# The second feed-forward layer's input half as seven products of quarters

## The chip, the cores and the metric

The kernel runs on one core of one Trainium2 chip. The metric is the device time of one execution in microseconds (us). The core has a matrix engine (TensorE, PE in the profile; PEld is its loading of stationary operands), a vector engine (VectorE, DVE), an activation engine (ScalarE, ACT), GpSimd (POOL) and a queue that starts transfers (SyncE, SP). SBUF is the working memory of 128 partitions; PSUM, eight banks of 128 x 512 float32, takes what TensorE accumulates.

## The reference, cut to what matters

Two layers run over 512 latent tokens of width 1024. Each has a token mixer (layer 0 attention, layer 1 a chunked gMLP), then a gated feed-forward layer. The change touches the last of these, in layer 1:

```
FFN_HIDDEN = 2816
def swiglu(h, w_in, w_out):
    gate, up = jnp.split(h @ w_in, 2, axis=-1)
    return (jax.nn.silu(gate) * up) @ w_out
...
f_l = swiglu(modulate(rmsnorm(x, norm_g[i, 2]), sh_fl, sc_fl), ffn_w_in[i], ffn_w_out[i])
x = x + g_fl * rmsnorm(f_l, norm_g[i, 3])
```

## The kernel before

**Numbers.** Every large product keeps float32 accuracy by three fp32r matmuls. An operand is split into a high part, `high`, a cast on ACT (L195), and a low part, `low`, the difference on DVE (L198). The three products are hi·hi, hi·lo and lo·hi.

**The feed-forward layer's input half** (class `FFN`). The hidden width 2816 is 22 units of 128 columns. A unit's weights are 128 gate and 128 up columns for all 1024 inputs: one raw tile of 1 MB (`w_raw`, two buffers), fetched by SP, and split in two halves into `w_hi` and `w_lo` (four buffers each). `H` holds the layer's input turned to features x tokens, high parts in its first eight blocks and low parts in its last eight. Units 0 and 1 (weight units 55 and 56) are done token by token in `head`, while the mixer's output product still runs. Units 2 to 21 (weight units 57 to 76) are done in `rest`: for gate and for up, eight blocks of 128 inputs, three matmuls of 512 tokens each (L1302, L1303, L1304), so 48 matmuls a unit. `gated` takes the silu on ACT (L1282) and multiplies on DVE (L1283). A background generator `ada` builds one modulation vector during the first of these units: eight multiply-adds on DVE (L335), two broadcast sums on PE.

**What comes before and after.** `down` is an output product with its norm and residual chain: for each of the four token tiles it ends with `work` for the last weight units, then the `Chain` steps: square on ACT, gain (L1096), add to x (L1100), the gain for the next layer on POOL (L1112), shift on DVE (L1116), `turn` on PE (L1123), and the turned tile split into `H` on ACT and DVE. `head` (L239 to L241, `fa`) and `head_turn` (L1276, L1277) are laid among these steps. Two calls matter: the mixer's `down(GO, ...)`, which leads into the feed-forward layer, and the last `down`, the output half, which follows it and ends the program.

**What sets the order.** Inside `down` the steps are registered with `at(time, step)`, and `run_plan` issues them in the order of a hand-kept list of names, `ORDER`, or, for steps it does not name, by that time. The times are places in an order only. Each engine then works its own queue in that order, and semaphores between the engines hold the dependences. In `rest` the order is that of the code.

Of the kernel before, what the change touches and what calls it, by code (L numbers as in the profile page):

```python
# [181 lines left out]
def backbone_kernel(ctx: ExitStack, tc: tile.TileContext, a, out):  # L182
# [46 lines left out]
    def big(name):  # L229
        return base.tile([P, 2 * D], F32, name=name, tag="big", bufs=2)  # L230

# [86 lines left out]
    class Ada:  # L318
# [14 lines left out]
        def add(self, k, c0=0, c1=D):  # L333
            w, ac = self.raws[k // 2][:, (k % 2) * D + c0:(k % 2) * D + c1], self.acc[:, c0:c1]
            nc.vector.scalar_tensor_tensor(out=ac, in0=w, scalar=sc[:, k:k + 1], in1=ac, op0=ALU.mult, op1=ALU.add)  # L335

# [723 lines left out]
    def slot(name):  # L1060
        return psM_p.tile([P, D], F32, name=name, tag="b2", bufs=4)
# [76 lines left out]
    def down(u0, nu, lhs, G_of, nxt_of, head, bg=None, lend=None, part={}, yslot=lambda t: slot(f"y{t}")):  # L1138


        ps, sts = {}, {}
# [9 lines left out]
        def work(v, t, ns=(0, 1)):  # L1151
            v0 = 2 if t in part else 0
            if v < v0:
                return
            if v == v0:
                ps[t] = yslot(t)
            parts = ws.unit(u0 + v)
            for h in range(2):
                k = 2 * v + h
                st = sts[k]  # L1160
                mm_a(ps[t], st[:, t * P:(t + 1) * P], st[:, 512 + t * P:512 + (t + 1) * P], *parts[h],
                     k == 2 * v0, k == nk - 1, ns)

        ws.unit(u0)
# [16 lines left out]
        for t, c in enumerate(ch):  # L1181
            b = W * (t + 1)
            if nxt is None and t == NT - 1:
# [19 lines left out]
            if nxt is None:  # L1203
                at(b + 3.7, c.store)
                continue
# [5 lines left out]
        if nxt is not None:  # L1211
# [10 lines left out]
            for i in range(6):  # L1222
# [3 lines left out]
                at(b + 1, ws.low, u, h, nc.vector)  # L1226
        with tc.manual_schedule():
            run_plan()
    class FFN:
# [55 lines left out]
        def rest(self, nxt_of, head, bg=None):  # L1285
            H, prev = self.H, None
            if head is None:
                psM.__exit__(None, None, None)
                psE = pool("psE", space=PSUM)
                pe = psE.__enter__()  # L1290
                self.slot = lambda name: pe.tile([P, D], F32, name=name, tag="b2", bufs=3)
                self.bank = lambda name: pe.tile([P, 512], F32, name=name, tag="b1", bufs=2)
# [30 lines left out]
            if head is None:  # L1323
                down(F2[self.layer], NFF // 2, lhs, lambda: V[self.layer, 5], nxt_of, head, yslot=lambda t: (
                    self.slot(f"y{t}") if t < NT - 1 else tuple(self.bank(f"y{t}{n}") for n in range(2))))
                psE.__exit__(None, None, None)
            else:
                down(F2[self.layer], NFF // 2, lhs, lambda: V[self.layer, 5], nxt_of, head, bg, self.lend)
# [144 lines left out]
    f1 = FFN(1, ada(1, (5,), lambda name: f1.bank(name)))  # L1473
# [7 lines left out]
    down(GO, 4, lambda k: staged(uTs[k]), lambda: V[1, 2], lambda: (V[1, 4], V[1, 3], H2), f1.head, lend=open_f1)  # L1481
    f1.rest(lambda: None, None)
# [80 lines left out]
```

## Time and profile before

| | us |
|---|---|
| median of 3 runs (1169.78 to 1170.39) | 1169.95 |
| the profiled execution, its own time | 1170.17 |
| its span in the profile | 1168.4 |
| PE busy in the span | 1152.3 |
| DVE, ACT, POOL busy | 647.5, 450.4, 192.0 |
| the mixer's `down` with `head`, about | 785 to 823 |
| input half of the last feed-forward layer, units 2 to 21 | 823.04 to 1042.08 |
| its output half | 1042.08 to 1162 |
| end of the last chain and stores | 1162 to 1168.4 |

A row of a timeline gives a start, a duration, the engine, the line and the operation with its tile names; a square bracket gives the idle time before it and what ended it. Matmuls are pipelined: their own durations overlap, so the time one costs is read from start to start.

### The profile page before, as it was taken

The numbers are of one execution on the slowest core, as the hardware profiler recorded it, in microseconds if no ns is written. First come the engines' busy times: TensorE is split into PE (matmuls) and PEld (weight loads), VectorE is DVE, ScalarE is ACT, GpSimd is POOL, SyncE is SP. The second block draws the span as 40 slices with busy tenths as digits, with TensorE's granted clock in tenths as the row PEclk, the third lists the DMA queues.
The fourth block names the chain that finished last, engine by engine and source line by source line (L and its number), as shares of the span: only waits on it lengthen the run. The fifth ranks groups of instructions, "written<-read, shape, count | busy, mean of one in ns | idle before, by whom it ended". The sixth has DMA issues, their size and how long they took to land.

```text
span 1168.4 us, 14727 instructions
## 1 busy us (share of the span) xinstructions
PE 1152.3 (99%) x5918; PEld 954.8 (82%) x5918; DVE 647.5 (55%) x915; ACT 450.4 (39%) x723; POOL 192.0 (16%) x181
## 2 busy tenths in 40 slices
PE   8999999999999999999999999999999999999997
PEld 5789887778988888888888788889788888888886
DVE  6778989857454657634445755547453223223324
ACT  6357778655222222332324454245122222222322
POOL 2347576515000000000001322013000000000000
PEclk9999999999999999999999999999999999999999
DMA  9633222341254575633344243221352232232221
GB/s 370 264 134 124 85 97 73 109 172 63 99 195 175 185 284 216 250 111 127 125 144 144 95 159 126 73 72 73 134 218 95 95 108 94 87 108 94 87 72 72
DMA packets 24711, 157.97 MB, mean 135 GB/s; under 512 B 3258, under 2 KB 3514, under 8 KB 7364
## 3 DMA queue, kind: packets, MB, share of 16 engines
q1 hardware_dynamic: 24644, 157.04, 37.3%
q8 instruction: 46, 0.75, 0.3%
q14 instruction: 21, 0.17, 0.0%
HBM read 154.94 MB, written 2.10 MB: 134 GB/s over the span
## 4 chain that ended last, share of the span: by engine, by line
PE 91%; DVE 3%; DMA 2%; POOL 1%; ACT 1%; issue 1%; DVEq 0%; POOLq 0%; SPq 0%; ACTq 0%
PE y L247 25%; PE f L1302 12%; PE f L1304 12%; PE f L1303 12%; PE v L247 3%; PE o_ps L915 2%; PE pT_ps L895 2%; DMA ada<-in_ada 2%; PE s_ps L861 2%; PE s_ps L862 1%; PE q_ps L239 1%; PE u L1454 1%; PE u L1456 1%; PE u L1455 1%; PE q_ps L241 1%; PE q_ps L240 1%
## 5 line engine op out<-in xcount | busy, mean ns | idle before, releaser
L198 DVE TENSOR_TENSOR w_lo<-w_raw,w_hi 128x1024 fp32r<-128x1024 f32 x149 | 182.2, 1230 | 319.0 <-ACT w_hi L195 317.4
L195 ACT CAST w_hi<-w_raw 128x1024 fp32r<-128x1024 f32 x162 | 168.6, 1052 | 469.8 <-PE f L1303 247.1
L1302 PE MATMUL f<-H,w_hi 128*128 128x512 f32 x640 | 249.5, 390 | 1.5 <-DVE act L1277 1.5
L247 PE MATMUL y<-w_hi,st 128*128 128x512 f32 x928 | 250.9, 390 | 0.0
L1304 PE MATMUL f<-H,w_lo 128*128 128x512 f32 x640 | 249.1, 389 | 0.0
L1303 PE MATMUL f<-H,w_hi 128*128 128x512 f32 x640 | 249.0, 389 | 0.0
L247 PEld LDWEIGHTS y<-w_hi,st 128*128 128x128 f32 x928 | 173.7, 188 | 35.9
L247 PE MATMUL y<-w_lo,st 128*128 128x512 f32 x464 | 143.5, 389 | 0.0
L335 DVE SCALAR_TENSOR_TENSOR acc<-ada_raw,sc,acc 128x1024 f32<-128x1024 f32 x80 | 104.5, 1306 | 69.9 <-DMA ada_raw<-in_ada 68.8
L1302 PEld LDWEIGHTS f<-H,w_hi 128*128 128x128 f32 x640 | 120.1, 188 | 26.5 <-DVE act L1277 1.7
L1304 PEld LDWEIGHTS f<-H,w_lo 128*128 128x128 f32 x640 | 120.1, 188 | 25.1
L1303 PEld LDWEIGHTS f<-H,w_hi 128*128 128x128 f32 x640 | 120.2, 188 | 25.0
L223 POOL TENSOR_TENSOR ry<-ry,mhalf 128x1 f32<-128x1 f32 x16 | 10.1, 633 | 584.3 <-DVE ry L220 580.9
L247 PEld LDWEIGHTS y<-w_lo,st 128*128 128x128 f32 x464 | 87.1, 188 | 18.1
L889 POOL TENSOR_SCALAR p<-p,st 128x512 f32<-128x512 f32 (+1 forms) x64 | 55.8, 888 | 43.9 <-DVE st L885 26.6
L868 DVE CUSTOM_DVE_ANT_0 s_ps<-s_ps,mask,nsink 128x512 f32<-128x512 f32 (+1 forms) x64 | 51.8, 816 | 11.5 <-PE s_ps L862 9.2
L873 ACT ACTIVATE p<-s_ps,st 128x512 f32<-128x512 f32 (+1 forms) x64 | 47.6, 744 | 20.6 <-DVE st L868 16.9
L198 POOL TENSOR_TENSOR w_lo<-w_raw,w_hi 128x512 fp32r<-128x512 f32 (+1 forms) x23 | 37.8, 1653 | 29.5 <-ACT w_hi L195 29.5
L326 POOL MEMSET acc<- 128x1024 f32 x10 | 9.5, 955 | 201.8 <-DVE acc_st L198 200.3
L895 PE MATMUL pT_ps<-ident,p 128*128 128x128 f32 x288 | 42.3, 274 | 0.0
L861 PE MATMUL s_ps<-khi,qT 128*128 128x256 f32 (+1 forms) x128 | 40.8, 330 | 1.5 <-ACT p L873 0.8
L1112 POOL TENSOR_TENSOR tmp<-x,row 128x1024 f32<-128x1024 f32 x12 | 31.8, 2650 | 32.7 <-DVE x L1100 24.9
(208 smaller groups left out, 1679.5 us busy)
## 6 DMA issues: line engine op xcount, KB each, us to landing
w_raw<-in_w SPq DMA_DIRECT2D x87, 1024.0 KB, 4.8
ada_raw<-in_ada SPq DMA_DIRECT2D x40, 1024.0 KB, 4.8
ada<-in_ada SPq DMA_DIRECT2D x8, 1024.0 KB
row<-in_norm_g SPq DMA_DIRECT2D x7, 512.0 KB, 5.6
xin<-in_x SPq DMA_DIRECT2D x4, 512.0 KB, 5.7
x<-in_x SPq DMA_DIRECT2D x4, 512.0 KB, 3.9
out<-x SPq DMA_DIRECT2D x3, 512.0 KB, 2.6
xin<-in_ctx SPq DMA_DIRECT2D x2, 512.0 KB
```

What stands on the lines that cost most here:

```text
L195: nc.scalar.copy(out=hi, in_=src)
L198: (eng or nc.vector).tensor_tensor(out=lo, in0=src, in1=hi.bitcast(F32), op=ALU.subtract)
L247: nc.tensor.matmul(dst, l, w[:, n * 512:(n + 1) * 512], start=first and i == 0, stop=last and i == 2)
L335: nc.vector.scalar_tensor_tensor(out=ac, in0=w, scalar=sc[:, k:k + 1], in1=ac, op0=ALU.mult, op1=ALU.add)
L861: nc.tensor.matmul(dst, self.qT[:, j, :], khi[:, self.g, k0:k0 + (c1 - c0) * P], start=True, stop=False)
L868: nc.vector.tensor_tensor_reduce(out=s, in0=s, in1=self.msk, scale=-1.0, scalar=nsink[:, h:h + 1], op0=ALU.add, op1=ALU.min, accum_out=sel ...
L873: nc.scalar.activation(out=p[:, 0:self.n], in_=self.s[j], func=AF.Exp, scale=-1.0, bias=self.st[:, 4 + j:5 + j], accum_out=self.st[:, 8 + ...
L889: nc.gpsimd.tensor_scalar(out=p, in0=p, scalar1=self.st[:, 12 + j:13 + j], scalar2=1.0, op0=ALU.mult, op1=ALU.mult)
L895: nc.tensor.transpose(ps[:, j * P:(j + 1) * P], self.probs[j][:, i * P:(i + 1) * P], ident)
L1302: nc.tensor.matmul(dst, hi, H[:, k, :], start=k == 0, stop=False)
L1303: nc.tensor.matmul(dst, hi, H[:, KC + k, :], start=False, stop=False)
L1304: nc.tensor.matmul(dst, lo, H[:, k, :], start=False, stop=k == KC - 1)
```

## The change

Units 2 to 21 of the input half are computed by seven products of quarters. The inputs (1024) are halved, giving weight quarters B11 (first half, gate), B12 (first half, up), B21 and B22; and the tokens (512) are halved, giving A11, A12 (second half of the inputs), A21 (second half of the tokens) and A22. With

S1 = A21 + A22, S2 = S1 - A11, S3 = A11 - A21, S4 = A12 - S2 and T1 = B12 - B11, T2 = B22 - T1, T3 = B22 - B12, T4 = B21 - T2

the seven products are P1 = A11·B11, P2 = A12·B21, P3 = S4·B22, P4 = A22·T4, P5 = S1·T1, P6 = S2·T2, P7 = S3·T3. Gate is P1+P2 for the first tokens and P1+P6+P7+P4 for the second; up is P1+P6+P5+P3 and P1+P6+P7+P5. Each product is four blocks of 128 inputs, three matmuls of 256 tokens each.

What is new in the code:

- In `down(GO, ...)`, by `prepare`: the four sums S of the inputs. A11 and A12 are put together again from `H` on POOL (`rebuild`); the sums are formed on DVE, partly out of PSUM (`sum_a`); each is split (`sum_high`, `sum_low`). The differences T of unit 57 and its four parts are prepared there too. `ORDER` lists this stretch anew.
- In `seven`, for each unit: four differences T on POOL (`diff`, 128 x 512 each); four parts split on ACT and DVE (`part_high`, `part_low`: part 0 is B11, 1 is T1 and T2, 2 is B21 and B22, 3 is T3 and T4); 84 matmuls; three copies out of PSUM on ACT (`keep`); three additions with one PSUM operand on DVE (`gate1`, `up1`, `up2`); two silus and one multiplication (`gates`). P4 of a unit is laid in the next unit.
- The modulation vector is fetched in eight chunks of 512 KB, into other buffers, one chunk every second unit (`fetch_chunk`, `add_chunk`).
- Before the last unit's P4, `lead` lays the first `work` of the output half. There, the first three chains square and gain in halves.

```
+        def rebuild(self, q, t):
...
+            nc.gpsimd.tensor_tensor(out=dst, in0=hi, in1=lo, op=ALU.add)
...
+        def sum_a(self, name, c):
...
+            out, in0, in1, op = {"S3": (s3, s1, a21, ALU.subtract), "S2": (s2, a22, s3, ALU.subtract),
+                                 "S1": (s1, s2, s1, ALU.add), "S4": (s4, s4, s2, ALU.subtract)}[name]
+            nc.vector.tensor_tensor(out=out, in0=in0, in1=in1, op=op)
...
+        def diff(self, n, i):
...
+            x, y, op = {1: lambda: (q("B12"), q("B11"), ALU.subtract), 3: lambda: (q("B22"), q("B12"), ALU.subtract),
+                        2: lambda: (T[3], q("B11"), ALU.add), 4: lambda: (q("B21"), T[2], ALU.subtract)}[i]()
+            nc.gpsimd.tensor_tensor(out=T[i], in0=x, in1=y, op=op)
...
+        def product(self, n, i):
...
+            for k in range(4):
+                w = slice(c0 + k * step, c0 + k * step + P)
+                for j, (l, r) in enumerate(((whi, ahi), (whi, alo), (wlo, ahi))):
+                    nc.tensor.matmul(dst, l[:, w], r[:, k, :], start=first and k == 0 and j == 0,
+                                     stop=k == 3 and j == 2, skip_group_check=True)
...
+        def seven(self):
...
+            T, last, u0 = 10.08, NFF - 1, self.u0
+            at(.1, self.head_turn, *self.prev)
+            for n in range(2, NFF):
+                b = T * (n - 2)
+                order = (1, 5, 4, 6, 2, 3, 7) if n > 2 else (1, 2, 5, 6, 3, 7)
+                for i, p in enumerate(order):
+                    at(b + T / 7 * i, self.product, n - 1 if p == 4 else n, p)
+                at(b + 1.7, self.keep, n, 0)
...
+                at(b + 7.45, self.gate1, n)
+                at(b + 9, self.up1, n)
+                at(b + T + .3, self.up2, n)
...
+                at(b + T + 5.3, self.gates, n)
+                if n < last:
+                    for i, j in enumerate((1, 3, 2, 4)):
+                        at(b + .02 + 1.28 * i, self.diff, n + 1, j)
+                    for i, hi, lo in ((0, 2.1, 2.8), (1, 5, 6.2), (2, 6.6, 7.9), (3, 8.9, T + .8)):
+                        at(b + hi, self.part_high, n + 1, i)
+                        at(b + lo, self.part_low, n + 1, i)
...
+                at(T * (1 + 2 * k) + 5, m5.fetch_chunk, k)
+                at(T * (3 + 2 * k) + 9.6, m5.add_chunk, k)
...
+                at(b, work, 0, 0)
+                at(b + 2.88, self.product, last, 4)
...
-    f1 = FFN(1, ada(1, (5,), lambda name: f1.bank(name)))
+    f1 = FFN(1, None)
...
-    f1.rest(lambda: None, None)
+         also=f1.prepare)
+    f1.seven()
```

PE at the end of `head` (`fat` is its last turn), in the program before: the first unit's matmuls follow at once, 48 of them, each of 512 columns.

```order
L1276 MATMUL fat<-ident,silu_a 128x128 x2
L1302 MATMUL f<-H,w_hi 128x512
L1303 MATMUL f<-H,w_hi 128x512
L1304 MATMUL f<-H,w_lo 128x512
L1302 MATMUL f<-H,w_hi 128x512
L1303 MATMUL f<-H,w_hi 128x512
L1304 MATMUL f<-H,w_lo 128x512
```

PE at the same place in the changed program, where the lines have other numbers (L1456 is `product`, L1308 the turn): P1, then `head`'s last turn, then P2 and the start of P5.

```order
L1308 MATMUL fat<-ident,silu_a 128x128 x2
L1456 MATMUL f_7102<-H,x_6847 128x256 x12
L1308 MATMUL fat<-ident,silu_a 128x128 x2
L1456 MATMUL f_7122<-H,w_hi 128x256 x2
L1456 MATMUL f_7122<-H,w_lo 128x256
L1456 MATMUL f_7122<-H,w_hi 128x256 x2
L1456 MATMUL f_7122<-H,w_lo 128x256
L1456 MATMUL f_7122<-H,w_hi 128x256 x2
L1456 MATMUL f_7122<-H,w_lo 128x256
L1456 MATMUL f_7122<-H,w_hi 128x256 x2
L1456 MATMUL f_7122<-H,w_lo 128x256
L1456 MATMUL f_7141<-S,w_hi 128x256 x2
```

So 48 matmuls of 512 columns a unit became 84 of 256, and P2 stands behind `w_lo`, the low of part 2.

DVE ahead of the same place, before, from the last two tiles' lows into `H` on (L1267 is `head`'s gated product, L1277 its copy, L198 `low`).

```order
L198 TENSOR_TENSOR H<-hT,H 128x4x128 x2
L1267 TENSOR_TENSOR silu_a<-fa,silu_a 128x256
L1277 COPY act<-fat 128x2x128
L198 TENSOR_TENSOR w_lo<-w_raw,w_hi 128x1024 x3
L1267 TENSOR_TENSOR silu_a<-fa,silu_a 128x256
L1277 COPY act<-fat 128x2x128
```

And in the changed program (L200 is `low`, L1389 `sum_a`, L1299 the gated product, L1309 the copy).

```order
L1389 TENSOR_TENSOR a_sum<-a_sum 128x4x128
L1299 TENSOR_TENSOR silu_a<-fa,silu_a 128x256
L1309 COPY act<-fat 128x2x128
L1389 TENSOR_TENSOR a_sum<-a_sum 128x4x128
L200 TENSOR_TENSOR S<-a_sum,S 128x1024
L1299 TENSOR_TENSOR silu_a<-fa,silu_a 128x256
L1309 COPY act<-fat 128x2x128
L200 TENSOR_TENSOR S<-a_sum,S 128x1024
L1299 TENSOR_TENSOR silu_a<-fa,silu_a 128x256
L1309 COPY act<-fat 128x2x128
L200 TENSOR_TENSOR w_lo<-w_raw,w_hi 128x1024
L200 TENSOR_TENSOR w_lo<-T,w_hi 128x1024
```

The sums S and two of their lows now stand ahead of the low that P2 waits for; three lows of weights stood there before.

POOL in the same stretch of the changed program (L1375 is `rebuild`, L1420 `diff`, L1126 the chain's gain); before, only the gain and the small L225 steps stood there.

```order
L1375 TENSOR_TENSOR a_sum<-H 128x4x128
L1126 TENSOR_TENSOR tmp<-x,row 128x1024
L225 TENSOR_TENSOR rx<-rx,mhalf 128x1
L1375 TENSOR_TENSOR a_sum<-H 128x4x128 x2
L1420 TENSOR_TENSOR T<-w_raw 128x512 x2
L1420 TENSOR_TENSOR T<-T,w_raw 128x512
L1375 TENSOR_TENSOR a_sum<-H 128x4x128
L1420 TENSOR_TENSOR T<-w_raw 128x512 x2
L1420 TENSOR_TENSOR T<-w_raw,T 128x512
L1420 TENSOR_TENSOR T<-T,w_raw 128x512
L1420 TENSOR_TENSOR T<-w_raw,T 128x512
```

Four rebuilds, the last chain's gain and the eight differences of two units now follow each other on POOL.

## Rows read from the trace of the kernel before

**Rows 1.** The page: PE's busy time and its share of the span.

```profile
PE 1152.3 (99%) x5918; PEld 954.8 (82%) x5918; DVE 647.5 (55%) x915; ACT 450.4 (39%) x723; POOL 192.0 (16%) x181
```

**Rows 2.** Windows: stretch, its length, busy time by engine, granted clock, DMA share, GB/s.

```profile
785.00:821.00 36.00, 36.00 (x269) 34.18 (x268) 26.82 (x39) 18.33 (x29) 12.13 (x9) 1.00 0.16 60
...
823.00:1042.00 219.00, 218.96 (x966) 181.22 (x967) 74.50 (x75) 53.45 (x64) 0.00 (x0) 1.00 0.33 118
1042.00:1162.00 120.00, 119.92 (x530) 98.99 (x528) 42.29 (x48) 33.05 (x46) 1.64 (x3) 1.00 0.22 80
```

**Rows 3.** Timeline of PE: the input half's first and last matmuls.

```profile
823.04 0.50 PE L1302 MATMUL f<-H,w_hi 128*128 128x512 f32 x1 [1.49 <-DVE act L1277]
...
1034.83 0.39 PE L1303 MATMUL f<-H,w_hi 128*128 128x512 f32 x1
...
1041.85 0.39 PE L1304 MATMUL f<-H,w_lo 128*128 128x512 f32 x1
1042.08 0.61 PE L247 MATMUL y<-w_hi,st 128*128 128x512 f32 x2
```

**Rows 4.** Timeline of PE in `head`: matmuls of 256 columns, two from one run of them.

```profile
812.45 0.28 PE L240 MATMUL fa<-w_lent,H 128*128 128x256 f32 x1
...
817.96 0.28 PE L241 MATMUL fa<-w_lent,H 128*128 128x256 f32 x1
```

**Rows 5.** DVE by line and shape: count, busy us, mean ns of one, idle before.

```profile
L198 DVE TENSOR_TENSOR w_lo<-w_raw,w_hi 128x1024 fp32r<-128x1024 f32 x147 | 180.4, 1235 | 319.0 <-ACT w_hi L195 317.4 <-PE ada_ps L351 1.5
L335 DVE SCALAR_TENSOR_TENSOR acc<-ada_raw,sc,acc 128x1024 f32<-128x1024 f32 x80 | 104.5, 1306 | 69.9 <-DMA ada_raw<-in_ada 68.8
...
L1283 DVE TENSOR_TENSOR act<-f,silu 128x512 f32<-128x512 f32 x40 | 27.3, 683 | 0.0
...
L1116 DVE SCALAR_TENSOR_TENSOR tmp<-tmp,rx,row 128x512 f32<-128x512 f32 x24 | 17.1, 747 | 10.4 <-POOL rx L223 10.3
...
L198 DVE TENSOR_TENSOR H<-hT,H 128x512 fp32r<-128x512 f32 x24 | 15.7, 682 | 5.7 <-ACT H L195 5.6
...
L1267 DVE TENSOR_TENSOR silu_a<-fa,silu_a 128x256 f32<-128x256 f32 x8 | 3.4, 420 | 2.9 <-ACT silu_a L1266 2.9
```

**Rows 6.** Timeline of POOL at two places.

```profile
104.37 1.28 POOL L198 TENSOR_TENSOR acc_st<-acc,acc_st 128x512 fp32r<-128x512 f32 x1
105.60 1.28 POOL L198 TENSOR_TENSOR w_lo<-w_raw,w_hi 128x512 fp32r<-128x512 f32 x1
...
791.58 2.43 POOL L1112 TENSOR_TENSOR tmp<-x,row 128x1024 f32<-128x1024 f32 x1 [4.78 <-DVE x L1100]
...
797.89 3.23 POOL L1112 TENSOR_TENSOR tmp<-x,row 128x1024 f32<-128x1024 f32 x1 [2.86 <-DVE x L1100]
```

**Rows 7.** Timeline of DVE at the same places and ahead of the input half.

```profile
105.62 2.34 DVE L335 SCALAR_TENSOR_TENSOR acc<-ada_raw,sc,acc 128x1024 f32<-128x1024 f32 x1
...
797.63 1.22 DVE L198 TENSOR_TENSOR w_lent<-w_raw,w_lent 128x1024 fp32r<-128x1024 f32 x1
799.38 1.22 DVE L1096 TENSOR_TENSOR tmp<-y,row 128x1024 f32<-128x1024 f32 x1 [0.53 <-ACT junk L213]
...
805.11 1.28 DVE L1100 SCALAR_TENSOR_TENSOR x<-tmp,ry,x 128x1024 f32<-128x1024 f32 x1 [0.44 <-POOL ry L223]
...
818.84 3.49 DVE L198 TENSOR_TENSOR w_lo<-w_raw,w_hi 128x1024 fp32r<-128x1024 f32 x3
```

**Rows 8.** ACT by line and shape, columns as in rows 5.

```profile
L195 ACT CAST w_hi<-w_raw 128x1024 fp32r<-128x1024 f32 x162 | 168.6, 1052 | 469.8 <-PE f L1303 247.1 <-PE y L247 153.1 <-DMA w_raw<-in_w 27.7
L195 ACT CAST st<-act 128x512 fp32r<-128x512 f32 x44 | 26.9, 617 | 0.0
...
L1266 ACT ACTIVATE silu_a<-fa 128x256 f32<-128x256 f32 x8 | 3.1, 384 | 15.5 <-PE fa L241 15.5
```

**Rows 9.** The page's DMA issues: count, KB each, median us from issue to landing.

```profile
w_raw<-in_w SPq DMA_DIRECT2D x87, 1024.0 KB, 4.8
```

More of the change, by code (lines that the diff above doesn't have):

```diff
@@ L1136, in turned_lo, with down @@
             low(lo, hi, src)
[L1138 to L1141 removed]
+    def down(u0, nu, lhs, G_of, nxt_of, head, bg=None, lend=None, part={}, yslot=lambda t: slot(f"y{t}"),
+             lead=None, also=None):
+        ps, sts, done = {}, {}, set()
         nk = 2 * nu
@@ L1152, in work @@
             v0 = 2 if t in part else 0
-            if v < v0:
+            if v < v0 or (v, t, ns) in done:
                 return
+            done.add((v, t, ns))
             if v == v0:
@@ L1162, in work, with take @@
                      k == 2 * v0, k == nk - 1, ns)
+        def take(k):
+            sts[k] = lhs(k)
+        if lead is not None:
+            lead(take, work)
         ws.unit(u0)
@@ L1182, in down @@
             b = W * (t + 1)
-            if nxt is None and t == NT - 1:
+            if nxt is None and t < NT - 1:
+                at(W * t, work, nu - 2, t)
+                at(W * t + W / 2, work, nu - 1, t)
+                for n in range(2):
+                    cs = (n * 512, (n + 1) * 512)
+                    at(b + .6 * n, c.square_y, *cs)
+                    at(b + .4 + .7 * n, c.gain_y, *cs)
+                at(b + 1.2, c.rstd_y)
+                at(b + 2.65, c.add_x)
+                at(b + 3.7, c.store)
+                continue
+            if nxt is None:
                 for n in range(2):
@@ L1221, in down @@
             at(13, ws.fetch, end + 2)
-            for i in range(6):
+            for i in range(6 if also is None else 4):
                 u, h = end + i // 2, i % 2
@@ L1322, in rest @@
                 pass
[L1323 to L1326, printed above, removed]
-            else:
-                down(F2[self.layer], NFF // 2, lhs, lambda: V[self.layer, 5], nxt_of, head, bg, self.lend)
+            down(F2[self.layer], NFF // 2, lhs, lambda: V[self.layer, 5], nxt_of, head, bg, self.lend)
@@ new lines, in sum_high @@
+        def sum_high(self, name):
+            src = self.sums[name]
+            if name == "S4":
+                hi, lo = (base.tile([P, D], F32R, name="s4", tag="vec", bufs=6).rearrange("p (k s) -> p k s", k=4)
+                          for _ in range(2))
+            elif name != "S3":
+                s = self.p.tile([P, 8, 256], F32R, name="S", tag="S", bufs=2)
+                hi, lo = s[:, 0:4, :], s[:, 4:8, :]
+            if name != "S3":
+                self.A[name] = (hi, lo)
+            high(self.A[name][0], src)
@@ new lines, in keep, with up2, up1 @@
+        def keep(self, n, i):
+            if i == 0:
+                self.c[n] = base.tile([P, D], F32, name="fc", tag="stg", bufs=4)
+            nc.scalar.copy(out=self.c[n][:, i * 256:(i + 1) * 256], in_=self.ps[n, 1 if i == 1 else 0])
+        def up2(self, n):
+            c = self.c[n]
+            nc.vector.tensor_tensor(out=c[:, 768:], in0=self.ps[n, 0], in1=c[:, 256:512], op=ALU.add)
+        def up1(self, n):
+            c = self.c[n][:, 512:768]
+            nc.vector.tensor_tensor(out=c, in0=self.ps[n, 1], in1=c, op=ALU.add)
@@ new lines, in gate1, with silu, gates @@
+        def gate1(self, n):
+            ps = self.ps[n, 2]
+            nc.vector.tensor_tensor(out=ps, in0=ps, in1=self.c[n][:, 0:256], op=ALU.add)
+        def silu(self, n, i):
+            if i == 0:
+                self.g[n] = self.p.tile([P, SEQ], F32, name="silu", tag="silu", bufs=2)
+            nc.scalar.activation(out=self.g[n][:, i * 256:(i + 1) * 256], in_=self.ps[n, 0 if i else 2], func=AF.Silu)
+        def gates(self, n):
+            nc.vector.tensor_tensor(out=self.act(n), in0=self.c.pop(n)[:, 512:], in1=self.g.pop(n), op=ALU.mult)
```

154 lines of the change are left out of this document (132 added, 22 removed).

## The prediction, made before the changed kernel was run

> **What bounds the kernel now.** I read the page's busy times first: PE is busy for 1152.3 of 1168.4 us [rows 1]. Since matmuls overlap, that alone does not say that PE is the limit, so I went to the windows of the stretches concerned: in the input half DVE is busy for 74.5 of 219 us, ACT for 53.5, POOL not at all, and the granted clock is 1.00, the upper of its two levels (2.4 GHz) [rows 2]. Next the timeline of PE. The input half begins at 823.04 and its last matmul starts at 1041.85, the output half following 0.23 us later [rows 3]. The 31 steps from 1034.83 to 1041.85 take 7.02 us, so a matmul of 512 columns costs 0.2265 us; 960 of them (20 units of 48) are 217.4 of the stage's 219.04 us, the rest being four broadcast matmuls and a turn. Nothing waits there: PE's matmul count sets the time. Just ahead PE does wait, 1.49 us before the first matmul [rows 3], for DVE, which had three lows of weights (3.49 us from 818.84) in front of what PE needed [rows 7].
>
> **What the change removes and adds on PE.** 960 matmuls of 512 columns go, 20 x 84 = 1680 of 256 come. The columns fall by an eighth, but a matmul is not paid by columns alone. `head` already runs matmuls of 256 columns, each with its own load of 128 x 128: the 46 steps from 812.45 to 817.96 take 5.51 us, so one costs 0.1198 us [rows 4], not half of 0.2265. That prices the new stage at 1680 x 0.1198 = 201.3 us against 217.4: **16.1 us less**, 0.81 us a unit (10.06 against 10.87), of the 27 that an eighth would be. The operands' roles are swapped against `head` (weights are now loaded, inputs move), but types and sizes are the same, so I take that price without a margin.
>
> The Trainium skill (TensorE: Matmul & The Clock Gate, section Back-to-back issue gap) gives the isolated gap at full clock as N/2.4 + 2.5 ns, that is 216 ns for 512 columns and 109 for 256. By it a unit would fall from 10.36 to 9.18 us and the stage by about 24 us, an estimate from that page; the rows show 227 and 120 for these fp32r matmuls with a load each, and the rows decide.
>
> **What it adds beside PE, per unit of 10.06 us.** ACT: three casts of 1.052, one of 0.617, three copies and two silus priced by the silu of 128 x 256 at 0.384 [rows 8]: 5.7 us. DVE: three lows of 1.235, one of 512 columns 0.684 (as the lows into H at 0.682), the gated product 0.683, three additions with a PSUM operand at 0.42 [rows 5]: 6.3 us, and in every second unit from n = 5 to 19 a chunk of the modulation vector, 1.306, eight in all. POOL: four differences of 128 x 512 at 1.28 [rows 6]: 5.1 us. Transfers: 1 MB a unit as before, landing in 4.8 us [rows 9], and 512 KB every second unit. Each engine fits when alone.
>
> They are not alone, and this is the risk. At 105.60 POOL began a subtraction of two SBUF tiles; DVE began its multiply-add of SBUF tiles at 105.62 and took 2.34 us where its mean is 1.306, ending 1.08 us after POOL's end [rows 5 to 7]: it stood still while POOL worked. The other way round, a DVE low at 797.63 held POOL's gain of 797.89 for 0.8 us (3.23 against 2.43), while DVE's gain of 799.38, one operand in PSUM, took its usual 1.22 under the same POOL instruction [rows 6, 7]. So POOL's differences and DVE's operations with both operands in SBUF take turns. In a unit that is 4 x 1.28 + 3 x 1.235 + 0.684 + 0.683 = 10.2 us, or by the steps from start to start (1.23 on POOL from 104.37 to 105.60, (3.49 - 1.235)/2 = 1.13 for a low, about 0.6 for the halves) 4.92 + 3.39 + 1.2 = 9.5 us; with the chunks 10.0 on average by steps, 10.7 by durations. **PE needs 10.06.** These are nearly equal, so what decides is whether lateness reaches PE. Each part has room: part 1 of the next unit can be cast when P4 has freed its buffer, 4.3 us into a unit, and is needed 11.5 us into it; parts 2 and 3 become free at 5.8 and 8.6 and are needed at 15.8 and 18.7. A cast, a wait of one POOL instruction and a low are 3.5 us. And POOL restrains itself: its next differences want the next raw tile, whose buffer comes free with the low of part 2, 4.8 us before landing. Walking the two queues by these durations I get part 1 ready about 3 us ahead of PE in every unit, the chunk units included. I therefore take 0 for the steady units, with a range from 0 to 20 x 0.6 = 12 us (10.7 - 10.06, durations instead of steps).
>
> **The entry** (end of `head`, start of the products). Gone are the three lows of weights and PE's wait of 1.49 us. From the last chain's addition to the low of part 2, for which P2 waits, DVE now has that addition 1.28 [rows 7], four shifts 0.747, six lows into H 0.682, eight sums 0.68, four gated products and three copies 0.42, the low of part 0 at 0.684, and three lows of 1.235 (S2, S1, part 2) [rows 5]: 21.3 us. The addition stood at 805.11 before [rows 7]; the new order finishes the fourth tile's output product one turn and one `head` run earlier (at about 795), which puts it near 798.2, so without turns DVE is done at 819.5. PE's own work is unchanged to 821.3; P1 (1.44) and the turn follow, and P2's third matmul would ask at 823.1. So 3.6 us are to spare. Against them stand 13 POOL operations (four rebuilds, the gain, eight differences) and 13 DVE operations with both operands in SBUF. If every one cost DVE a wait, 12 x 1.28 + 2.43 = 17.8 us, PE would lose 14.2; if none did, nothing. Walking it, about half of them hit, as the list alternates with operations out of PSUM: DVE reaches that low some 9 us later by turns but gains back about 2.5 since its steps are shorter than its durations. PE then waits some 3.3 us in three places: before the last tile's turn, before `head`'s last turn, and in P2. Less the 1.49 removed, **1.8 us are added**; range -1.5 to +12.7.
>
> **The exit.** The first `work` of the output half is laid ahead of the last P4, 24 matmuls' worth of cover for copies and silus; without it the last gate would wait for a silu, an addition and a product, 0.384 + 0.42 + 0.683 = 1.5 us [rows 5, 8]. The halved squares and gains of the first three chains lie beside matmuls, and the last chain is unchanged: 0.
>
> **Sum**, against the profiled execution's own 1170.17 (0.2 above the median): 1170.2 - 16.1 + 1.8 = **1155.9 us**.
>
> **Rivals.**
> (a) *Taking turns reaches PE in part.* DVE works through its queue in order, so a waiting low holds the additions that free PSUM behind it, and ACT's next casts behind POOL. At 0.4 us a unit, 8 us go back: 1164. For it: demand and supply of the turn are within 6%. Against: the 3 us of room. Its outer end, all 12 us with 1.8 at the entry, is 1168, no longer distinguishable from no change.
> (b) *DVE becomes the bound: slower.* Each POOL difference finds DVE wanting two SBUF operands, and the PSUM additions stand in series too: 4.92 + 3.39 + 1.2 + 3 x 0.34 (steps) = 10.53, with 0.52 for chunks on average 11.05 a unit against 10.87 before, 20 x 0.18 + 1.8 = 5.4 us slower: 1175.5. It decides from 10.78 a unit on. For it: DVE's order is fixed and POOL's four differences form one chain. Against: it needs every difference to hit, although DVE spends three operations in each unit out of PSUM and waits for PE's results itself.
> Beside (a) and (b): the Trainium skill (SBUF — State Buffer, section Who interferes with whom) says that a DVE instruction with two SBUF inputs and a GpSimd instruction that reads SBUF exclude each other for a whole instruction, whoever begins first. The 2.34 and 1.22 us of rows 7 agree, and it speaks against putting sums on POOL to spare DVE; taken alone, without the room in the buffers, it would give the 1175.5 of (b).
> (c) *The entry costs nothing*: the sums fit the 3.6 us, and the old wait goes: 1170.2 - 16.1 - 1.5 = 1152.6.
>
> **Chances.** Forecast, with (c) as its lower end, 1152.5 to 1160: 0.64. Rival (a) from 1160 to 1167.8: 0.19. Within 0.2%, about what a measurement of this kernel can tell from no change (1167.6 to 1172.3): 0.06. Rival (b): 0.11. So faster 0.83, same 0.06, slower 0.11. The range for 8 in 10 runs from 1152.5 to 1166: it takes in the forecast and most of (a).
>
> **What the next profile would show.** Starts of the product's matmuls 0.120 us apart and units 10.06 to 10.1 us apart, the clock at 1.00: the gain is right. Idle rows of PE behind DVE or ACT between 808 and 830, about 3 us together: the entry is right; 8 or more, and the sums collide worse than walked. DVE lows of 1.2 us stretched to over 2 and POOL differences beyond 1.28: the turns are real; they cost nothing as long as PE shows no idle row in the units. Units of 10.5 us and more, PE waiting for lows of parts 1 or 3, would be (a) or (b). Wrong altogether would be matmuls spaced wider than 0.120, since the whole gain hangs on that price.

## The result and the profile after

The changed kernel takes **1157.88 us** (median of four executions, 1154.83 to 1160.60) against 1169.96 before (1169.78 to 1170.39): a ratio of 0.9896, 95% interval 0.9864 to 0.9927. In three later series beside the kernel before it took 1155.09, 1156.04 and 1155.62, ratios 0.9869, 0.9880 and 0.9872. Forecast were 1155.9 us and a range from 1152.5 to 1166. The profiled execution took 1155.57, with a span of 1153.8; all rows of "after" come from it. Three of its 16 executions in all lie near 1160; the last experiment shows where one of them loses its 5 us.

The page of the changed kernel (busy time of each engine, its share of the span, instructions) answers [rows 1]; two windows of it (stretch, length, busy time of PE, PEld, DVE, ACT and POOL, granted clock, DMA share, GB/s) answer [rows 2]:

```profile
PE 1135.3 (98%) x6638; PEld 974.6 (84%) x6638; DVE 771.0 (67%) x1030; ACT 507.6 (44%) x853; POOL 359.3 (31%) x265
```

```profile
785.00:821.00 36.00, 36.00 (x272) 34.33 (x271) 33.40 (x44) 16.78 (x29) 31.45 (x21) 1.00 0.09 30
826.00:1029.00 203.00, 201.27 (x1654) 199.64 (x1654) 182.80 (x176) 105.57 (x181) 145.75 (x73) 1.00 0.36 127
```

PE's busy time fell by 17.0 us, and the span by 14.6. In the products DVE has become nearly as full as PE, and POOL is no longer idle: they are busy for 182.8 and 145.8 of 203 us, where they had 74.5 and 0 of 219. The clock is at its upper level, as before.

PE's timeline at the start and the end of the products (start, duration, engine, line, operation, out<-in, count, and in brackets the idle time ahead and who ended it) answers [rows 3]:

```profile
820.54 1.68 PE L1456 MATMUL f<-H,x 128*128 128x256 f32 x12
822.06 0.38 PE L1308 MATMUL fat<-ident,silu_a 128*128 128x128 f32 x2
822.20 0.48 PE L1456 MATMUL f<-H,w_hi 128*128 128x256 f32 x2
823.69 0.39 PE L1456 MATMUL f<-H,w_lo 128*128 128x256 f32 x1 [1.01 <-DVE w_lo L200]
...
1025.67 0.40 PE L1456 MATMUL f<-H,w_hi 128*128 128x256 f32 x2
1025.91 0.28 PE L1456 MATMUL f<-H,w_lo 128*128 128x256 f32 x1
1026.03 1.32 PE L252 MATMUL y<-w_hi,st 128*128 128x512 f32 x5
```

The waits of PE from 785 us on, in the view of waits (who waits, for whom, us in total, times, longest):

```profile
PE f L1456 <- DVE fc L1467: 1.2, 2, 0.7
PE f L1456 <- DVE w_lo L200: 1.0, 1, 1.0
PE ada_ps L365 <- DVE acc_st L200: 0.5, 1, 0.5
```

Matmuls stand 0.12 us apart (two in 0.24, one in 0.12), as [rows 4] priced them. The 14.6 us of the span divide by three marks that both kernels have: the first wait for `qT` in the attention (79.65 us before, 79.08 after), the first product and the first matmul of the output half. Ahead of the first mark 0.6 us are gone, which is the start of the program and not the change. From there to the first product 1.9 are gone (743.39 to 741.46): 1.49 of them the removed wait. From the first product to the output half it was 219.04; it is 205.49, with the 1.44 of the last P4 that now lies behind that mark 206.9: 12.1 less. The price alone said 16.1 less, so 4.0 us came back as waits. The four idle stretches above are 2.7 us, but idle time is counted from a matmul's modelled end, and a wait costs more than that: the matmul behind the one of 823.69 starts at 823.91, where steps of 0.12 from 822.20 give 822.56, so 1.35 for an idle time of 1.01. By the same reckoning the waits in the units (834.30 and 865.46) cost 0.8 and 0.9, and that of the modulation vector's total (1007.88) 0.9: 4.0 in all. Three more profiles of this kernel lack the last of these waits; their stage is 204.6 to 204.7 us.

What PE waits for in the units is no low of a weight part but the addition `up2` (L1467): it reads the PSUM tile to which P4 adds next. At 865.46 it comes late because a chunk of the modulation vector (L348) stands right ahead of it on DVE:

```profile
863.09 1.98 DVE L348 SCALAR_TENSOR_TENSOR acc<-ada_k,sc,acc 128x1024 f32<-128x1024 f32 x1
864.99 0.41 DVE L1467 TENSOR_TENSOR fc<-f,fc 128x256 f32<-128x256 f32 x1
865.46 0.51 PE L1456 MATMUL f<-H,w_hi 128*128 128x256 f32 x2 [0.67 <-DVE fc L1467]
```

DVE by line and shape from 826 to 1029 us (count, busy us, mean ns of one, idle before and who ended it), against [rows 5], and POOL's differences, against [rows 6]:

```profile
L200 DVE TENSOR_TENSOR w_lo<-T,w_hi 128x1024 fp32r<-128x1024 f32 x39 | 71.2, 1825 | 3.4 <-ACT w_hi L197 3.3
L200 DVE TENSOR_TENSOR x<-w_raw,x 128x512 fp32r<-128x512 f32 x19 | 21.3, 1120 | 2.1 <-ACT x L197 1.9
L348 DVE SCALAR_TENSOR_TENSOR acc<-ada_k,sc,acc 128x1024 f32<-128x1024 f32 x8 | 15.8, 1978 | 0.0
L1475 DVE TENSOR_TENSOR f<-f,fc 128x256 f32<-128x256 f32 x20 | 8.4, 420 | 0.3 <-PE f L1456 0.3
```

```profile
L1420 POOL TENSOR_TENSOR T<-w_raw 128x512 f32<-128x512 f32 x36 | 69.2, 1942 | 36.2 <-DMA w_raw<-in_w 27.0 <-DVE x L200 6.8 <-DVE act L1483 2.2
L1420 POOL TENSOR_TENSOR T<-T,w_raw 128x512 f32<-128x512 f32 x18 | 38.0, 2108 | 1.4
```

A low of 1.235 us takes 1.825, one of 512 columns 1.120 in place of 0.684, a chunk 1.978 in place of 1.306; a difference on POOL takes 1.9 to 2.1 where one alone took 1.28. The additions with an operand in PSUM keep their 0.42. Those are the forecast turns: the wait for the other engine stands inside the instruction's duration, and no idle row shows it.

### The profile page after: what moved, and what is told of

Same layout as the page of the kernel before. It is cut to its first block, busy times and chain, and to the rows that moved or that the text cites. A ratio compares the mean times of both kernels' runs of the same rounds, so it can differ in the third digit from the quotient of the medians.

```text
span 1153.8 us, 16530 instructions
## 1 busy us (share of the span) xinstructions
PE 1135.3 (98%) x6638; PEld 974.6 (84%) x6638; DVE 771.0 (67%) x1030; ACT 507.6 (44%) x853; POOL 359.3 (31%) x265
## 4 chain that ended last, share of the span: by engine, by line
PE 84%; DVE 7%; POOL 2%; DMA 2%; issue 2%; ACT 2%; SPq 0%; DVEq 0%; POOLq 0%; ACTq 0%
PE y L252 25%; PE f L1456 13%; PE f L1328 6%; PE f L1330 6%; PE f L1329 6%; PE v L252 3%; PE o_ps L929 2%; PE pT_ps L909 2%; PE s_ps L875 1%; PE u L1690 1%; PE u L1692 1%; PE u L1691 1%; DVE w_lo L200 1%; POOL T L1420 1%; PE s_ps L876 1%
## 5 line engine op out<-in xcount | busy, mean ns | idle before, releaser
L200 DVE TENSOR_TENSOR w_lo<-w_raw,w_hi 128x1024 fp32r<-128x1024 f32 x129 | 171.4, 1336 | 182.9 <-ACT w_hi L197 181.4
L197 ACT CAST w_hi<-w_raw 128x1024 fp32r<-128x1024 f32 x142 | 147.8, 1051 | 308.6 <-PE y L252 140.1
L1328 PE MATMUL f<-H,w_hi 128*128 128x512 f32 x320 | 124.8, 390 | 0.0
L1330 PE MATMUL f<-H,w_lo 128*128 128x512 f32 x320 | 124.6, 389 | 0.0
L1329 PE MATMUL f<-H,w_hi 128*128 128x512 f32 x320 | 124.5, 389 | 0.0
L225 POOL TENSOR_TENSOR ry<-ry,mhalf 128x1 f32<-128x1 f32 x16 | 9.2, 577 | 368.1 <-DVE ry L222 228.6
L1456 PE MATMUL f<-H,w_hi 128*128 128x256 f32 x480 | 89.4, 284 | 1.2 <-DVE fc L1467 1.2
L1420 POOL TENSOR_TENSOR T<-w_raw 128x512 f32<-128x512 f32 x40 | 75.6, 1911 | 36.2 <-DMA w_raw<-in_w 27.0
L1456 PEld LDWEIGHTS f<-H,w_hi 128*128 128x128 f32 x480 | 74.9, 192 | 1.9 <-DVE fc L1467 1.6
L200 DVE TENSOR_TENSOR w_lo<-T,w_hi 128x1024 fp32r<-128x1024 f32 x40 | 72.4, 1809 | 3.4 <-ACT w_hi L197 3.3
L1330 PEld LDWEIGHTS f<-H,w_lo 128*128 128x128 f32 x320 | 60.1, 188 | 12.6
L1329 PEld LDWEIGHTS f<-H,w_hi 128*128 128x128 f32 x320 | 60.1, 188 | 12.5
L1328 PEld LDWEIGHTS f<-H,w_hi 128*128 128x128 f32 x320 | 60.1, 188 | 12.4
L1456 PE MATMUL f<-H,w_lo 128*128 128x256 f32 x240 | 68.0, 283 | 1.0 <-DVE w_lo L200 1.0
L1456 PE MATMUL f<-S,w_hi 128*128 128x256 f32 x320 | 59.3, 283 | 0.0
```

The lines of the kernel that those rows point to most:

```text
L197: nc.scalar.copy(out=hi, in_=src)
L200: (eng or nc.vector).tensor_tensor(out=lo, in0=src, in1=hi.bitcast(F32), op=ALU.subtract)
L1328: nc.tensor.matmul(dst, hi, H[:, k, :], start=k == 0, stop=False)
L1329: nc.tensor.matmul(dst, hi, H[:, KC + k, :], start=False, stop=False)
L1330: nc.tensor.matmul(dst, lo, H[:, k, :], start=False, stop=k == KC - 1)
L1420: nc.gpsimd.tensor_tensor(out=T[i], in0=x, in1=y, op=op)
```

## The experiments

**Theory**: POOL's differences and DVE's operations with two operands in SBUF take turns; in the changed kernel the turns just fit the 10.06 us that PE needs for a unit, so they cost PE almost nothing, and one more operation would cost its length. **Rivals**: the stretched durations are harmless and any such operation is absorbed; or POOL's work as such holds something up, turns or not. To compare the kernels closely I use, beside the medians, the stage from the first product to the output half in each profile, since it leaves out the start of the program: 204.7, 204.6 and 204.7 us in three more profiles of the changed kernel.

**The changed kernel again** (series one).

> The changed kernel once more, unaltered, beside the variants. Its four executions so far lay at 1154.8, 1155.6, 1160.2 and 1160.6 us, while the kernel before stays within 0.6 us. Theory (turns): POOL's differences and DVE's operations with two SBUF operands exclude each other, and how they fall differs from execution to execution, so that lateness reaches PE in some: times between 1154.5 and 1161 again, and where the profiled execution is one of the long ones, PE idles about 5 us more than the 2.7 us of the profile at hand, behind DVE or ACT in the units. Rival (transfers): late weight tiles make the difference; then the idle time in a long execution ends at transfers. Rival (clock): a lower granted clock on PE, with no idle rows.

1155.09 us (1154.79 to 1155.97), stage 204.7. None lay near 1160 this time, so the spread that this theory expected from the turns did not come; the last experiment takes it up.

**No differences in units 4 to 21.** The parts are split straight from the raw tile, so PE's work is the same and its data is not; what is left out is POOL's work alone.

```
 def source(self, n, i):
     if i == 0: return self.quarter(n, "B11")
+    if n > 3:
+        return ws.raws[self.u0 + n][:, (i > 1) * D:(i > 1) * D + D]
-            for i, j in enumerate((1, 3, 2, 4)):
+            for i, j in enumerate((1, 3, 2, 4) if n < 3 else ()):
```

> Left out: the four differences T of the weights for units 4 to 21 (18 of 20 units); the parts are split straight from the raw tile instead, so PE, ACT and DVE do the same work and POOL none in the units (the output is then not the product). Theory (turns): DVE's two-operand operations return to 1.2 us, PE idles only at the entry (1.0 us) and the time is 1152.5 to 1154.5 us with a spread under 1 us. Rival (transfers or clock make the spread): the same 5 us spread as the changed kernel, 1155 to 1160.

1153.38 us, 1.7 less than the changed kernel beside it; stage 202.6. The window of 180 us inside the stage, first of the changed kernel beside it, then of this kernel:

```profile
830.00:1010.00 180.00, 178.81 (x1483) 177.97 (x1483) 167.23 (x152) 92.92 (x160) 144.10 (x73) 1.00 0.36 130
830.00:1010.00 180.00, 180.00 (x1501) 179.92 (x1500) 119.44 (x156) 94.58 (x164) 0.00 (x0) 1.00 0.37 129
```

PE never stops, and DVE's 167.2 us have become 119.4: the lows are back at 1.22 us, so 48 us of DVE's busy time had been waiting. PE gains 1.7 us by the medians and 2.1 by the stage: that is what POOL's differences cost it. This kernel alone doesn't tell the turns from the lateness of the differences themselves; the next one makes the same differences without turns.

**The differences of units 4 to 21 on DVE.**

```
-            nc.gpsimd.tensor_tensor(out=T[i], in0=x, in1=y, op=op)
+            (nc.vector if n > 3 else nc.gpsimd).tensor_tensor(out=T[i], in0=x, in1=y, op=op)
```

> The differences of units 4 to 21 on DVE in the place of POOL, same order of steps. Theory (turns): a difference costs DVE 0.6 to 0.68 us instead of up to 1.28 us of waiting, so DVE's demand becomes 3.39 + 1.2 + 3 x 0.34 + 4 x 0.6 = 8.0 us a unit by steps, with chunks 8.5 on average, against PE's 10.06: 1152.5 to 1155 us, spread under 1.5 us, better than the changed kernel. Rival (DVE is the engine that is short, POOL relieves it): 9.1 us by durations plus a chunk of 1.3 in every second unit leaves no room for its waits, PE stalls on the lows, 1158 us or more.

1152.93 us, against the kernel before a ratio of 0.9856 (0.9837 to 0.9876); 2.2 less than with POOL beside it, stage 202.6. One of its four executions took 1156.30, beyond the spread that I expected; the profile is not of that one. The same window, and the differences by line and shape:

```profile
830.00:1010.00 180.00, 180.00 (x1500) 179.92 (x1499) 161.36 (x227) 94.63 (x163) 0.00 (x0) 1.00 0.36 129
```

```profile
L1420 DVE TENSOR_TENSOR T<-w_raw 128x512 f32<-128x512 f32 x36 | 24.6, 684 | 0.0
L200 DVE TENSOR_TENSOR w_lo<-T,w_hi 128x1024 fp32r<-128x1024 f32 x37 | 45.1, 1220 | 3.9 <-ACT w_hi L197 3.9
```

DVE does all the work of both engines in 161.4 us, less than its 167.2 with POOL's help, and PE does not wait there: so the turns, not the differences, cost the 2 us. A difference costs 0.69 on DVE and 1.28 on POOL, and while POOL has it DVE stands still for longer than it would have taken.

**A fifth subtraction on POOL, and a sixth.** One, then two, subtractions of raw quarters are added in each of units 4 to 21 behind the differences; the results are not used.

```
+        def extra(self, n):
+            q = base.tile([P, D], BF16, name="junk", tag="junk", bufs=1)[:, 0:512]
+            nc.gpsimd.tensor_tensor(out=q.rearrange("p (k m) -> p k m", k=4), in0=self.quarter(n, "B22"), in1=self.quarter(n, "B11"), op=ALU.subtract)
...
+                    if n > 2:
+                        at(b + 5.2, self.extra, n + 1)
```

> A fifth POOL subtraction of two raw quarters (128 x 512, SBUF operands, result unused) for units 4 to 21. Theory (turns): POOL and DVE together need 5 x 1.23 + 3.39 + 1.2 = 10.7 us a unit by steps, 11.3 on average with the chunks, above PE's 10.06, so 18 units grow by 0.7 to 1.4 us each: 1170 to 1185 us. Rival (each engine has its own time; POOL's 5 x 1.28 = 6.4 us fit in 10.06): no change, 1155 to 1160.

1167.37 us, ratio 0.9975 (0.9965 to 0.9986); stage 217.1, 12.5 longer, 0.69 us a unit. The window and PE's waits in this kernel:

```profile
830.00:1010.00 180.00, 169.62 (x1391) 167.26 (x1389) 174.84 (x143) 86.74 (x149) 168.01 (x85) 1.00 0.33 120
```

```profile
PE f L1460 <- DVE fc L1471: 8.1, 5, 1.7
PE f L1460 <- ACT fc L1467: 1.8, 1, 1.8
PE f L1460 <- DVE w_lo L200: 1.0, 1, 1.0
```

DVE is busy for 174.8 and POOL for 168.0 of the 180 us, and PE now waits for DVE's additions, the way rival (a) of the prediction described it: stretched operations hold the additions that free PSUM. All five of these waits (from 869 us on) lie in units with a chunk of the modulation vector; one of them, with DVE ahead of it (L1471 is `up2` here):

```profile
952.33 1.98 DVE L200 TENSOR_TENSOR w_lo<-w_raw,w_hi 128x1024 fp32r<-128x1024 f32 x1
954.57 1.97 DVE L348 SCALAR_TENSOR_TENSOR acc<-ada_k,sc,acc 128x1024 f32<-128x1024 f32 x1
956.46 0.41 DVE L1471 TENSOR_TENSOR fc<-f,fc 128x256 f32<-128x256 f32 x1
956.93 0.50 PE L1460 MATMUL f<-H,w_hi 128*128 128x256 f32 x2 [1.70 <-DVE fc L1471]
```

The added subtraction also reads the raw tile and could hold its buffer longer. That is not what costs: behind 855 us POOL waits for a raw tile three times, 1.5 to 1.8 us each, and nine times for 1.6 to 4.0 us in the changed kernel beside it.

The first rival, no change, falls. The theory's range began at 1170, so the time lies between the two ranges; the cost of 0.69 for an operation of 1.23 says that some room was still there. A second subtraction should tell:

> Two more subtractions of raw quarters on GpSimd in each of 18 units, results not used, so six in place of four. By the turns theory the turns had no room left with five (10.74 us a unit), so the sixth costs its full length of 1.23 to 1.28 us in each unit: 18 times that is 22 to 23 us more than with five, about 1190, slower than the kernel before the change. If with five only the order in GpSimd's queue held up the differences and the turns still had room, the sixth costs what the fifth did, 0.7 us a unit: about 1180.

1190.96 us, ratio 1.0176 (1.0159 to 1.0193), slower than the kernel before. The median speaks for a full turn, but this profile starts 5.3 us late (`qT` at 84.53), so I go by the stage: 236.2, 19.1 more than with five, 1.06 us a unit. That average takes in the first and the last units, which run differently. Between them PE's waits come in a fixed rhythm, here two of the kernel with five subtractions, then two of the kernel with six:

```profile
914.19 0.50 PE L1460 MATMUL f<-H,w_hi 128*128 128x256 f32 x2 [1.67 <-DVE fc L1471]
956.93 0.50 PE L1460 MATMUL f<-H,w_hi 128*128 128x256 f32 x2 [1.70 <-DVE fc L1471]
...
893.41 0.50 PE L1460 MATMUL f<-H,w_hi 128*128 128x256 f32 x2 [1.47 <-ACT fc L1467]
917.20 0.50 PE L1460 MATMUL f<-H,w_hi 128*128 128x256 f32 x2 [1.47 <-ACT fc L1467]
```

With five, four units take 42.74 us, 10.69 each; with six, two units take 23.79 us, 11.90 each; a unit without a wait takes 10.08. So the fifth costs 0.61 and the sixth 1.21, a full turn: the room was used up with the fifth. The theory's sums with the chunks, 11.3 and 12.5, are both 0.6 too high, so its step from one to the other was right and its start was not. Rival (b)'s point of 10.78 us a unit lies between the two: with five the kernel is still 2.7 us faster than before, with six it is 21 slower.

With six, PE also waits behind ACT, and POOL is the engine without time. The window of 180 us, and ACT's waits for POOL's differences in it:

```profile
830.00:1010.00 180.00, 160.13 (x1294) 156.07 (x1293) 157.96 (x132) 77.75 (x136) 166.96 (x88) 1.00 0.33 118
```

```profile
ACT w_hi L197 <- POOL T L1420: 42.5, 13, 4.0
```

POOL is busy for 167.0 us and waits 11.9 for raw tiles. Six operations of 1.28 would be 7.7 us a unit; beside DVE they take 1.5 to 2.2 each on average, by kind.

**POOL's work without reads.** In place of the two subtractions two settings to zero of 128x1024, in the same place.

```
-            nc.gpsimd.tensor_tensor(out=q.rearrange(...), in0=..., in1=..., op=ALU.subtract)
+            for _ in range(2):
+                nc.gpsimd.memset(base.tile([P, D], BF16, name="junk", tag="junk", bufs=1), 0.0)
```

> Two settings of a 128x1024 tile to zero on GpSimd in each of 18 units, which read nothing from SBUF, in the place where the two extra subtractions stood. If it is the reads of two operands from SBUF that make GpSimd and VectorE take turns, VectorE's operations keep their length (lows near 1.8 us) and the time stays at 1155 to 1157. If any work on GpSimd at that place holds the differences up, or any access to SBUF takes a turn, it is like one extra subtraction or worse: 1167 or more.

1156.22 us, stage 205.7, some 1 us over the changed kernel's (which ran beside other kernels, not beside this one). The window, POOL in it by line and shape, and DVE's lows:

```profile
830.00:1010.00 180.00, 178.07 (x1475) 176.98 (x1474) 154.59 (x151) 92.35 (x160) 170.74 (x107) 1.00 0.36 130
```

```profile
L1420 POOL TENSOR_TENSOR T<-w_raw 128x512 f32<-128x512 f32 x36 | 68.4, 1918 | 11.7 <-DMA w_raw<-in_w 11.7
L1424 POOL MEMSET junk<- 128x1024 bf16 x34 | 32.3, 951 | 1.0
```

```profile
L200 DVE TENSOR_TENSOR w_lo<-T,w_hi 128x1024 fp32r<-128x1024 f32 x36 | 53.3, 1480 | 4.0 <-ACT w_hi L197 4.0
```

32.3 us more of POOL's time cost 1 us, where 31.7 us of the fifth subtraction cost 12.5. I expected lows near 1.8 us, as in the changed kernel; they are 1.48, and DVE is busy for 154.6 us in place of 167.2, probably because these 0.95 us pass without a turn. It is the reading of operands in SBUF that counts, not that POOL is busy: here the second rival falls. This is also what the Trainium skill states (SBUF — State Buffer, section Who interferes with whom): a DVE instruction with two SBUF inputs contends with a GpSimd instruction that reads SBUF, not with one that only writes it. The rows agree on both sides: 12.5 us for the subtraction, 1 us for the settings to zero.

**The order at the entry.** DVE's low of part 2, for which PE waits 1.01 us at 823 us, ahead of the low of the sum S1.

```
-... sum_low#2 head_2_2#2 sum_low part_high_2_1 head_3_1#2 head_3_2#2 part_low_2_2 sum_high#3 ...
+... sum_low#2 head_2_2#2 part_low_2_2 part_high_2_1 head_3_1#2 head_3_2#2 sum_low sum_high#3 ...
```

> One swap in DVE's order at the entry of the last FFN: the low part of the second combination of unit 2, for which TensorE waited 1.01 us at 823 us, stands ahead of the low part of a sum of weights, where it stood behind head_3_2 before. If that wait is the whole price of the entry, the kernel takes 1.0 us less than the changed kernel (about 1154.1) and no wait shows at 823. If the wait comes from DVE's work as a whole and not from its order, the wait moves to the low part that now comes later (the sum's, which the fifth product of unit 2 asks for) and the time stays within 0.3 us.

1156.74 us against 1156.04 for the changed kernel beside it (next run), stage 205.9 against 204.6. PE's waits in the entry of this kernel, in its timeline:

```profile
825.38 0.39 PE L1456 MATMUL f<-S,w_lo 128*128 128x256 f32 x1 [0.72 <-DVE w_lo L200]
830.22 0.39 PE L1456 MATMUL f<-H,w_hi 128*128 128x256 f32 x1 [0.39 <-DVE H L200]
834.15 0.39 PE L1456 MATMUL f<-S,w_lo 128*128 128x256 f32 x1 [0.53 <-DVE w_lo L200]
837.04 0.50 PE L1456 MATMUL f<-H,w_hi 128*128 128x256 f32 x2 [1.45 <-DVE fc L1467]
```

The wait at 823 is gone and has come back in four smaller or later ones, 3.1 us in all (2.2 in the changed kernel beside it): 1.0 less was wrong. The other expectation named the right kind, a wait that moves, but not the size (the stage is 1.3 us longer) nor the place: the first wait is for the low of part 1, not for that of the sum, which is one of inputs and not of weights. DVE has no idle time there (9.00 us busy of the 9 from 821 to 830), so here the order only chooses which product waits.

**The changed kernel again** (series two, with the swap, the sixth subtraction and the next kernel).

> The changed kernel unaltered, as the measure for the three kernels beside it: 1155 to 1156 us. Its first profile came from runs at 1155 and 1160; none of 1160 came in the second series, so none is expected here.

1156.04 us (1154.76 to 1156.97), stage 204.6.

**The swap and the differences on DVE together.**

> The swap and the four differences of units 4 to 21 on VectorE instead of GpSimd, both together. Taken from the changed kernel: 1.0 us for the swap and 1.2 us for TensorE's short waits in the units (the kernel with the differences on VectorE alone kept TensorE busy for all of 830 to 1010 us): about 1152.2 to 1153.2, faster than both kernels. If the two remove the same wait, it stays at the 1153 of the differences alone.

1152.88 us (1152.28 to 1153.06), ratio 0.9853 (0.9838 to 0.9867), stage 202.3: the same as with the differences on DVE alone. It beats both kernels, as that one does; the swap takes 0.3 us off the stage, no more.

**No differences in the entry.** The eight of units 2 and 3 are left out, and those units' parts split from the raw tile; all others stay.

> The eight differences of units 2 and 3, which GpSimd makes while the entry runs, are left out (these units' parts are split straight from the raw tiles, so their products are not the weights' ones); all the others stay. If the 1.01 us that TensorE waits at 823 us come from turns with these differences, VectorE's four sums of 1.07 to 1.23 us go back to 0.68 and its three lows of 1.65 to 1.88 to about 1.23, 3.5 us in all, the wait vanishes and the time is 1.0 us less than the changed kernel beside it; the 1.1 us in the next units stay or vanish with it (1.0 to 2.1 less). If the wait is for the amount of VectorE's own work, it stays, and so does the time within 0.3 us.

1158.95 us, 3.3 more than the changed kernel beside it: neither theory. The stage is 206.4 against 204.7, so only 1.7 of the 3.3 come from the products. In the entry the turns of DVE's sums and lows are gone: a sum of inputs that took 1.07 to 1.23 us takes 0.68, the lows 1.22, and PE's wait there is 0.29 in place of 1.01. But 3.2 us of waits appear in the units behind it, where the changed kernel has 1.1; the entry's wait and the longest:

```profile
826.55 0.39 PE L1458 MATMUL f<-H,w_lo 128*128 128x256 f32 x1 [0.29 <-DVE w_lo L200]
854.09 0.50 PE L1458 MATMUL f<-H,w_hi 128*128 128x256 f32 x2 [1.62 <-ACT fc L1465]
```

A side effect of my edit is the likely reason: a part split from the raw tile keeps that tile until the low of part 3, and POOL's differences of unit 5 begin 23.9 us after the first product (848.00 - 824.12) where the changed kernel beside it has 22.7 (848.46 - 825.80). So the run shows that 0.7 of the 1.0 us of idle time come from turns, and leaves open what the entry's turns cost the whole.

**The changed kernel a fourth time.**

> The changed kernel unaltered, as the measure beside it: 1155 to 1157 us. If its profile falls on one of the executions near 1160 (2 of 12 so far), it shows where these lose the time: in the units behind VectorE if the turns fall differently there, elsewhere if not.

1155.62 us, and the profile fell on an execution of 1159.99. Its waits from 785 us on and its stage (204.7) are those of the others. So here it is not the turns that make the long execution, against the theory in the first repeat. It is late from the start: `qT` at 84.33 in place of 79.08 to 79.79, and from there to the end of the span 1073.9 us, against 1073.7 in the execution of 1154.76. Windows of the first 40 us, of this execution:

```profile
28.00:30.00 2.00, 2.00 (x12) 1.58 (x9) 2.00 (x2) 0.62 (x2) 2.00 (x1) 1.00 0.99 404
30.00:32.00 2.00, 0.32 (x2) 0.00 (x0) 2.00 (x3) 0.41 (x1) 0.74 (x1) 1.00 0.41 163
32.00:34.00 2.00, 1.86 (x19) 1.50 (x23) 1.93 (x7) 1.97 (x2) 0.84 (x1) 0.99 0.93 390
34.00:36.00 2.00, 2.00 (x14) 1.07 (x4) 2.00 (x1) 1.11 (x3) 2.00 (x2) 0.50 1.02 432
```

PE waits 1.82 us for a transposed tile of DVE from 30.3 on, and from 34 on its clock is granted at the lower of its two levels (0.50) for some 3 us, with matmuls of 512 columns 0.43 us apart; in 10 to 20 us there is another such stretch (0.83 on average). The code there is the same in both kernels. Three other profiles with a late `qT` (81.13 with five subtractions, 84.53 with six, 82.87 without the differences of the entry) have the same wait of 1.8 us, and the latter two also a stretch at the lower clock from 31 or 32 us on; none of the others has either. Why DVE is late there in some executions stays open.

## Why the prediction was right

**The price of a matmul: right.** 0.120 us apart; the kernel without differences had one wait, of 1.35 us, in its stage of 202.6: with the last P4's 1.44 and without the wait that is 202.7, against 201.3 + 1.6 = 202.9 by the prediction's sum.

**The steady units: right in kind, short by 2.6 us.** I took 0, as the turns (9.5 us a unit by steps) would fit 10.06 with about 3 us of room for each part. The turns are there and fit: from 870 to 1006 us PE shows no idle row. PE lost 1.7 us in units 3 and 6 and 0.9 at a total of the modulation vector, 2.6 in all; the three repeats lost the 1.7 alone. My walk followed the lows of the parts, and PE never waited for these in the units. It left out the additions out of PSUM, which rival (a) names: `up2` came late for P4, behind a low of 1.98 us in unit 3 and behind a chunk of 1.98 us in unit 6. At the first units POOL had waited 6.13 and 5.46 us for raw tiles and then ran its differences without a pause (from 843.3 to 863 us); that this is what delays DVE's additions there I only argue, no run takes it alone. The fifth subtraction shows how near the edge that was: rival (a) begins one POOL operation further on.

**The entry: the mechanism right, the term too large.** I expected 3.3 us of waits in three places; there was one, in P2, which cost 1.35. The walk put DVE's low of part 2 some 6.5 us behind the 819.5 of a DVE without turns (its terms add up to 21.1 us, not 21.3, so 819.3). It ended at 823.63 in a profile whose `qT` is 0.6 earlier: 4.7 behind 819.5 by the same mark. The first two places, the last turns, did not wait at all: DVE's shifts stretched to 1.79, 1.63, 1.77 and 0.98 us, and the transposes behind them were not late. The removed wait of 1.49 was as read. The two errors, the entry 2.0 too large and the units 2.6 too small, nearly cancel: waits of 4.0 - 1.5 = 2.5 us against 1.8 forecast, and 0.6 us at the start of the program hide the rest. That 1155.9 lies so near the profiled 1155.57 is therefore partly luck; the price of the matmul and the small size of the waits are not.

**The exit: right.** The output half begins 0.12 us behind the last product, without a wait, and the last P4 lies in it at 1033.77.

**Rival (b)** was a real case: its point of 10.78 us a unit lies between one POOL operation more (10.69) and two (11.90).

## What to carry to other kernels

Before work goes from DVE to GpSimd, count the operations of both that read two operands from SBUF and add them up in one queue per unit; here the sum of 10.0 us with the chunks cost the bounding engine's 10.06 almost nothing, and 11.3 cost 0.6 a unit. The fullest unit counts, not the average: here most of PE's waits behind DVE fell in the units with a chunk. GpSimd's price counts in the sum (1.28 us for what DVE does in 0.69). DVE alone had room for everything and was the better place, which its own busy share before (74.5 of 219 us) already allowed to see. The order swap, on an engine without idle time, mostly moved the wait.

## What of the hardware I had not expected

While DVE and POOL alternate, a POOL operation costs DVE more than the POOL operation's work is worth: 144 us of POOL's busy time in the window raised DVE's from 119 to 167, more than the 42 that the differences cost on DVE itself. And settings to zero on POOL (0.95 us each) take no turn: with 32 us of them in the window DVE's busy time was 154.6 us, less than the 167.2 without them.
